# Six edits to the order of work in a transformer layer: the end of the output stage, the norm tiles, one head's queue, and the token sums

## The chip, the cores and the metric

The kernel runs on one core of a Trainium2 chip. The core has a matrix engine (PE, TensorE), three engines for element-wise work (DVE or VectorE, ACT or ScalarE, POOL or GpSimd), and SP, whose queue issues the transfers between the outer memory and the core's own. Each engine takes its instructions strictly in the order of its own queue; an instruction that waits for a result of another engine holds up everything queued behind it. The metric is the device time in microseconds (us), the median of three runs: 1238.08 for the kernel before (1235.4 to 1239.1).

## The reference

One encoder layer on a sequence of 1024 tokens of width 1024. A projection of `x` is split between four mLSTM heads (a short convolution over tokens on q and k, then a recurrent matrix memory, both directions summed) and eight windowed attention heads; the head outputs go through one output projection; a first layer norm; a gated feed-forward network (SwiGLU, inner width 2816) with a gated extra embedding; a second layer norm.

```python
mix = concat([mlstm(conv(x @ Wqk), x @ Wv), attention(x @ Waq)]) @ w_out
x   = layer_norm(ALPHA * x + mix, ln1_g, ln1_b)
ffn = (silu(x @ Wg) * (x @ Wu)) @ w_ffn_out
x   = layer_norm(ALPHA * x + ffn + sigmoid(x @ Wple_g) * (p @ Wple_p), ln2_g, ln2_b)
```

## The kernel before, in words

All products are made to fp32 accuracy from two-part operands: a high part that ACT rounds off (`split`: `act.copy`) and a low part, the rest, that POOL or DVE subtracts. `mm3` makes hi*hi, lo*hi and hi*lo into one PSUM bank, so a 128x512 product of 128x128 weights is three PE instructions. Where names below end in h and l (`mh`, `ml`, `a1h`, `a1l`, `t3h`, `t3l`) they are such parts.

The 1024 tokens are eight tiles of 128. The stages are: projections of x; attention; four mLSTM heads one after the other (each works in 128-token chunks on PE, with long chains over ACT, POOL and DVE between the products, while the PE queue is filled up with projection products of the next head); the output projection; the first norm (`ln1_*`) tile by tile, tiles 4 to 7 before 0 to 3 (`TORD`); the feed-forward network by a two-by-two block scheme with 7 products for 8, which needs sums of pairs of tiles (`t_sums`: tile t+4 += tile t; `t_sums2`: the sums of the second kind, formed from those in place, by two additions on the engine named); its output (`run_out`, `ffn_out`) and the second norm (`ln2`).

In the second norm DVE collects the statistics, POOL raises the variance to the power -1/2 (`rs`, a 128x1 instruction), DVE subtracts the mean and multiplies by the gain, and each half row is then finished either by one DVE instruction (times `rs`, plus the bias `b2b`) or by ACT (times `rs`) and POOL (plus `b2b`), and sent out by SP.

Most of the program is placed by a scheduler: it builds each engine's queue from its own estimate of when things are ready. `strict[0]` and `fixed[0]` keep a stretch in the written order, and `with tc.issue_after(ins)` puts instructions into their engine's queue behind `ins`; on the same engine that is an order and no wait. In the output stage (`ffn_out`) each block `m` is the sum of six weight pieces for four tiles; the last block (`m == 4`, tiles 0 to 3) is run tile by tile, the one before it (`m == 3`, tiles 4 to 7) piece by piece over all four.

The names that matter below: `ks` (scaled keys of a head chunk), `kp` (keys transposed by PE), `pp` (query-key product), `qk` (a convolved q or k, five DVE instructions over 1024 tokens: one TENSOR_SCALAR and four SCALAR_TENSOR_TENSOR), `hs` (a head's output chunk), `tr` (its transpose on PE), `so` (the output of a head, normed), `yo` (a PSUM bank of the output projection), `y` (a norm tile, `y_4121`, `4149`, `4169`, `4185` for tiles 0 to 3 and `3960`, `4007`, `4050`, `4085` for 4 to 7), `rg` and `ru` (raw feed-forward weights) and `x_8193` to `x_8199` (odd; output tiles 0 to 3).

Of the kernel before, what the change touches and what calls it, by code (L numbers as in the profile page):

```python
# [10 lines left out]
ALU = mybir.AluOpType  # L11
# [4 lines left out]
P = 128  # L16
D = 1024
S = 1024
# [17 lines left out]
def hybrid_layer(  # L36
# [80 lines left out]
    def pjb(name):  # L117
        return pj.tile([P, 512], F32, name=name, tag="pj")

    def flat(t):  # L120
        return t.rearrange("p a b -> p (a b)")

    def split(dst_hi, dst_lo, src, eng_lo=None):
        act.copy(dst_hi, src)
        if eng_lo == "halves":
            for c in range(2):
                cs = slice(c * 512, c * 512 + 512)
                pool.tensor_tensor(dst_lo[:, cs], src[:, cs], dst_hi[:, cs].bitcast(F32), ALU.subtract)
            return
        (eng_lo or pool).tensor_tensor(dst_lo, src, dst_hi.bitcast(F32), ALU.subtract)  # L130

    def load_w(src, shape, name, eng_lo=None, raw=None):
# [4 lines left out]
        lo = wp.tile([P] + shape, F32R, name="lo_" + name, tag="wlo", bufs=4)  # L137
        split(flat(hi), flat(lo), flat(raw), eng_lo or "halves")
        return hi, lo

    last = {}

    def mm3(o, ah, al, bh, bl, start, stop, goes_on=False):
        pe.matmul(o, ah, bh, start=start, stop=False, skip_group_check=goes_on)
# [36 lines left out]
    def drain(n=0):  # L181
        while len(fillers) + len(running) > n:
            fill(1)
# [120 lines left out]
    def qk_tile(ct):  # L304
        def evac(o, hf):
            if hf == 0:
                pre = qk["pre", ct] = prep.tile([P, S + 4], F32, name="pre", tag="pre")
                dve.memset(pre[:, 0:2], 0.0)
                dve.memset(pre[:, S + 2:S + 4], 0.0)
            pre = qk["pre", ct]  # L310
            act.copy(pre[:, 2 + hf * 512:514 + hf * 512], o)
            if hf == 1:
                y = qk[ct] = Y([P, S], F32, f"qk{ct}")
                dve.tensor_scalar(y, pre[:, 0:S], colt[:, ct, 0:1], colt[:, ct, 5:6], ALU.mult, ALU.add)
                for w in range(1, 5):
                    dve.scalar_tensor_tensor(y, pre[:, w:w + S], colt[:, ct, w:w + 1], y, ALU.mult, ALU.add)
                act.activation(y, y, AF.Silu)

        return proj_T(wqk[ct], f"qk{ct}", evac)
# [268 lines left out]
    def mlstm_head(h):  # L588
# [8 lines left out]
        for hf in range(2):  # L597
            kp_ = bank("kp", "ma")
            for cc in range(4):
                c = hf * 4 + cc  # L600
                pe.transpose(kp_[:, cc * P:(cc + 1) * P], kT[:, c * P:(c + 1) * P], ident)
            for d in range(2):
                kk = W([P, 4, P], F32, f"ks{d}{hf}", 4, "ks")
                if d == 0:
                    for cc in range(4):
                        r = col(d, hf * 4 + cc)
                        act.activation(kk[:, cc, :], kp_[:, cc * P:(cc + 1) * P], AF.Copy, scale=cWA[:, r:r + 1])
                else:
                    r = col(d, hf * 4)
                    dve.tensor_tensor(kk, kp_.rearrange("p (c k) -> p c k", k=P),  # L610
                                      cWA[:, r:r + 4].unsqueeze(2).to_broadcast([P, 4, P]), ALU.mult)
                ks[d, hf] = kk
            fillr()
        orders = (list(range(8)), list(range(7, -1, -1)))
# [137 lines left out]
    gated(MH - 1, last["mm"])  # L752
    for hf in range(2):
        finish(MH - 1, hf)
    drain()

    scope_s.close()
# [150 lines left out]
    for t in range(6):  # L908
        for nh in range(2):
            list(out_proj(t, nh, (0, 1), u, False))  # L910
            if (t, nh) in TR1:
                ln1_tr(TR1[t, nh])
            if (t, nh) == (3, 1):
                ws = [wino_w1(0, raw8), wino_w1(1, raw8f)]
                s2 = [wino_s(0, *ws[0][:2])]
                p2 = X([P, 8, P], F32R, "a20")
                split(p2[:, LO, :], p2[:, UP, :], ws[0][0][:, UP, :])
                p2 = p2[:, LO, :], p2[:, UP, :]
                s2.append(wino_s(1, *ws[1][:2]))
        if t < 5:  # L920
            ln1_norm(t)
# [218 lines left out]
    ln1_gain(7)  # L1140
    t_sums(1)
    t_sums2(0, dve)
    t_sums2(1, pool)

    def wlo(pr, sl, src, eng):
        eng.tensor_tensor(pr[1][:, sl, :], src, f32(pr[0][:, sl, :]), ALU.subtract)

    wlo(p3, UP, ru[:, LO, :], pool)
    rg1, ru1 = ws[1][:2]
    q2, q3 = w_pair(1, 2), w_pair(1, 3)  # L1150
    parts = (q2, LO, s2[1]), (q3, UP, ru1[:, LO, :]), (q2, UP, rg1[:, UP, :]), (q3, LO, ru1[:, UP, :])
# [6 lines left out]
    ob[1] = m12(1, 2, pjb("mb"))  # L1158
    t_sums(2)
    t_sums(3)  # L1160
    for t in (2, 3):
        t_sums2(t, pool)
    for part in ((p4, UP, s2[0]), (p4, LO, rg[:, LO, :]), (p3, LO, ru[:, UP, :])) + parts:
        wlo(*part, pool)
    evac([tr_pe((4, 5), 512, q) for q in range(2)], bx["t3"], 0, bdif)
# [13 lines left out]
    act.activation(hs[0][0], hs[0][0], AF.Silu)  # L1179
    oc = bank("mc", "w")  # L1180
    prod(w2[0], 5, oc, True)
    tb = tr_pe((6, 7), 512, 1)
    tr_hi(tb, 1, bx["t3"], 2, bdif)
    tr_lo(tb, 1, bx["t3"], 2, bdif)
    act.activation(hs[1][0], hs[1][0], AF.Silu)
# [164 lines left out]
        nc.sync.dma_start(xb[:, :nj, :], hb[q][HB[m]][:, :nj, :])  # L1350
        return piece(new_pair, xa, nj, f"wo{m}{q}", dve), piece(new_pair, xb, nj, f"ho{m}{q}", dve), nj

    def run_out(o, units, first, tts=range(4)):
        for ui, (a, b, nj) in enumerate(units):
            for j in range(nj):
                for tt in tts:
                    s = slice(tt * P, (tt + 1) * P)
                    mm3(o[tt], b[0][:, j, s], b[1][:, j, s], a[0][:, j, :], a[1][:, j, :],
                        first and ui == 0 and j == 0, ui == len(units) - 1 and j == nj - 1, not first)

    def ffn_out():
        for t in range(NT):
            stat[t] = W([P, 2, 6], F32, "st2", 8)
        oa = [bank(f"oa{tt}", "w") for tt in range(4)]
        ob = None
        dst = {1: (0, 0), 2: (0, 0), 6: (0, 1), 5: (1, 1), 7: (1, 1), 3: (0, 1), 4: (1, 0)}
        for m in (1, 2, 6, 5, 7, 3, 4):
            if m in (2, 5):
                ob = [pjb(f"ob{m}{tt}") if tt < 3 else bank(f"ob{m}{tt}", "w") for tt in range(4)]
            o = ob if m in (2, 5, 3) else oa  # L1370
            units = [unit(m, q) for q in range((NPR + 1) // 2)]
            first = m in (1, 2, 5)
            if m != 4:
                run_out(o, units, first)
            nh, hf = dst[m]
            for tt in range(4):
                if m == 4:
                    run_out(o, units, first, [tt])
                y, t = yv(nh, hf, tt), hf * 4 + tt
                add(y, y, o[tt])  # L1380
                if m in (2, 7, 3, 4):
                    dve.bn_stats(stat[t][:, nh, :], y)
                if m in (3, 4):
                    ln2(t)

    def ln2(t):
        y = ya[t]
        mv = W([P, 2], F32, "mv2", 4)
        rs = W([P, 1], F32, "rs2", 4)
        dve.bn_aggr(mv, stat[t])  # L1390
        dve.tensor_scalar(rs, mv[:, 1:2], LN_EPS, None, ALU.add)
        pool.tensor_tensor(rs, rs, mhalf[:, 0:1], ALU.pow)
        dve.scalar_tensor_tensor(y, y, mv[:, 0:1], g2b, ALU.subtract, ALU.mult)
        for nh in range(2):
            ns = slice(nh * 512, nh * 512 + 512)
            if t >= 4 and nh == 0 or t == 7:
                dve.scalar_tensor_tensor(y[:, ns], y[:, ns], rs, b2b[:, ns], ALU.mult, ALU.add)
            else:
                act.activation(y[:, ns], y[:, ns], AF.Copy, scale=rs)
                pool.tensor_tensor(y[:, ns], y[:, ns], b2b[:, ns], ALU.add)  # L1400
            nc.sync.dma_start(out[t * P:(t + 1) * P, ns], y[:, ns])
# [74 lines left out]
```

## Time and profile before

| quantity | us |
|---|---|
| median of three runs | 1238.08 |
| profiled execution | 1238.7 |
| span of its trace | 1236.9 |
| PE busy | 1204.0 (97%) |
| DVE busy | 843.7 (68%) |
| ACT busy | 509.9 (41%) |
| POOL busy | 405.9 (33%) |
| PE's waits for other engines, summed | 21.3 |

The span is the traced time from first to last instruction; 1.8 us of the profiled execution lie outside it. Busy shares are averages over stages; what an edit is worth has to be read at its place, from the timeline there: one line is an instruction, or several alike, with start, busy time, engine, what it writes and reads, and in brackets how long its engine stood idle before it and for whom.

### The profile page before, as it was taken

The numbers are of one execution on the slowest core, as the hardware profiler recorded it, in microseconds if no ns is written. First come the engines' busy times: TensorE is split into PE (matmuls) and PEld (weight loads), VectorE is DVE, ScalarE is ACT, GpSimd is POOL, SyncE is SP. The second block draws the span as 40 slices with busy tenths as digits, with TensorE's granted clock in tenths as the row PEclk, the third lists the DMA queues.
The fourth block names the chain that finished last, engine by engine and source line by source line (L and its number), as shares of the span: only waits on it lengthen the run. The fifth ranks groups of instructions, "written<-read, shape, count | busy, mean of one in ns | idle before, by whom it ended". The sixth has DMA issues, their size and how long they took to land.

```text
span 1236.9 us, 16505 instructions
## 1 busy us (share of the span) xinstructions
PE 1204.0 (97%) x6017; PEld 1004.4 (81%) x6017; DVE 843.7 (68%) x1543; ACT 509.9 (41%) x920; POOL 405.9 (33%) x324
## 2 busy tenths in 40 slices
PE   8999999999999999899999999999999999999996
PEld 8888888788778878788888888888887888888885
DVE  6866555867788789665857667576467696555566
ACT  5655444534662236533324334333243333333331
POOL 4542322615344034622332323323227440000017
PEclk9999999999999999999999999999999999999998
DMA  6331112313174132145545454465345556565603
GB/s 233 94 97 69 44 60 79 130 35 121 51 243 167 51 137 102 35 133 177 183 164 196 168 190 163 145 220 180 126 137 208 192 187 224 193 194 189 187 1 136
DMA packets 68785, 174.40 MB, mean 141 GB/s; under 512 B 7328, under 2 KB 12128, under 8 KB 68704
## 3 DMA queue, kind: packets, MB, share of 16 engines
q1 hardware_dynamic: 68704, 173.35, 41.1%
q8 instruction: 47, 0.77, 0.3%
q14 instruction: 34, 0.28, 0.1%
HBM read 126.86 MB, written 46.47 MB: 140 GB/s over the span
## 4 chain that ended last, share of the span: by engine, by line
PE 77%; DVE 9%; DMA 2%; issue 2%; POOL 2%; ACT 2%; POOLq 0%; SPq 0%; ACTq 0%; DVEq 0%
PE ma L73 19%; PE mc L73 9%; PE oa L73 7%; PE ob L73 7%; PE pj_qk L73 6%; PE mb L73 4%; PE pg L73 4%; PE yo L73 3%; PE pn_v L73 3%; PE pj_o L73 2%; PE pj_aq L73 2%; PE op L73 2%; PE nd L73 2%; PE et L77 1%; PE sp L73 1%
## 5 line engine op out<-in xcount | busy, mean ns | idle before, releaser
L57 POOL TENSOR_TENSOR rs<-rs,mhalf 128x1 f32<-128x1 f32 (+1 forms) x24 | 22.0, 917 | 250.2 <-DVE rs L57 242.0
L57 POOL TENSOR_TENSOR s<-ru,rg 128x512 f32<-128x512 f32 x20 | 26.8, 1342 | 188.3 <-DMA ru<-in_wffi_dram 188.3
L57 POOL TENSOR_SCALAR e<-e,st 128x384 f32<-128x384 f32 (+1 forms) x64 | 35.0, 560 | 93.8 <-DVE st L57 54.8
L57 DVE TENSOR_TENSOR us<-us,ma 128x512 f32<-128x512 f32 x22 | 15.0, 683 | 68.3 <-PE ma L73 68.3
L73 PE MATMUL yo<-hi_wo,mh 128*128 128x512 f32 x128 | 51.5, 402 | 2.7 <-DVE y L57 2.7
L57 DVE SCALAR_TENSOR_TENSOR qk<-pre,colt,qk 128x1024 f32<-128x1024 f32 x32 | 52.4, 1636 | 0.6
L73 PE MATMUL pj_qk<-xh,hi_qk 128*128 128x512 f32 x128 | 51.5, 402 | 0.0
L73 PE MATMUL pj_qk<-xl,hi_qk 128*128 128x512 f32 x128 | 50.7, 396 | 0.0
L73 PE MATMUL pj_qk<-xh,lo_qk 128*128 128x512 f32 x128 | 50.6, 396 | 0.0
L73 PE MATMUL yo<-lo_wo,mh 128*128 128x512 f32 x128 | 50.2, 392 | 0.0
L73 PE MATMUL yo<-hi_wo,ml 128*128 128x512 f32 x128 | 49.7, 392 | 0.0
L57 ACT CAST a4h<-s 128x512 fp32r<-128x512 f32 x21 | 13.1, 622 | 84.5 <-POOL s L57 42.9
L57 POOL TENSOR_TENSOR s<-rg,s 128x512 f32<-128x512 f32 x20 | 26.4, 1320 | 56.1 <-DVE a4l L57 56.1
L57 ACT CAST a2h<-s 128x512 fp32r<-128x512 f32 x41 | 24.4, 619 | 49.2 <-PE mc L73 31.3
L57 DVE CUSTOM_DVE_ANT_0 e<-sp,bias 128x384 f32<-128x384 f32 (+1 forms) x64 | 31.2, 521 | 19.7 <-PE sp L73 17.8
L57 POOL TENSOR_TENSOR s<-ru 128x512 f32<-128x512 f32 x20 | 34.2, 1709 | 23.4 <-DVE a2l L57 23.4
L57 ACT ACTIVATE e<-e,st 128x384 f32<-128x384 f32 (+1 forms) x64 | 37.2, 583 | 8.3 <-DVE st L57 8.3
L57 ACT COPY eT<-et 128x384 f32<-128x384 f32 (+1 forms) x32 | 14.4, 450 | 54.5 <-PE et L77 54.4
L57 DVE TENSOR_TENSOR yb<-yb,us 128x512 f32<-128x512 f32 x22 | 36.3, 1651 | 0.0
L57 ACT ACT_TABLE_LOAD x25 | 32.1, 1283 | 9.1 <-DMA mw<-mwd 7.1
L73 PE MATMUL mc<-t1h,a3h 128*128 128x512 f32 x88 | 34.4, 391 | 0.8 <-DVE t1l L57 0.8
L73 PE MATMUL mb<-b21h,a1h 128*128 128x512 f32 x88 | 34.3, 390 | 0.0
(890 smaller groups left out, 4161.1 us busy)
## 6 DMA issues: line engine op xcount, KB each, us to landing
fb<-hb SPq DMA_DIRECT2D x35, 512.0 KB, 4.5
rg<-in_wffi_dram SPq DMA_DIRECT2D x22, 512.0 KB, 3.6
ru<-in_wffi_dram SPq DMA_DIRECT2D x22, 512.0 KB, 5.2
fa<-sb SPq DMA_DIRECT2D x20, 512.0 KB, 3.4
mw<-mwd SPq DMA_DIRECT2D x16, 512.0 KB, 5.3
fa<-in_wffo_dram SPq DMA_DIRECT2D x15, 512.0 KB, 3.8
hb<-yc SPq DMA_DIRECT2D x11, 512.0 KB, 2.9
hb<-ya SPq DMA_DIRECT2D x11, 512.0 KB, 3.7
```

Source lines behind the costliest of these rows:

```text
L57: self.ins = op(*args, **kw)
L73: return pe.put(nc.tensor.matmul(*args, **kw))
L77: return pe.put(nc.tensor.transpose(*args, **kw))
```

## The change: six edits

1. The cast of the first feed-forward weights (`a1h`, in `wino_w1`) is put into ACT's queue behind the last head's last cast (`mh`).
2. The five convolution instructions of the third `qk` tile are put into DVE's queue behind the last scale of keys (`ks`) of the first head that DVE makes.
3. The second kind of token sums of tile 1 goes from POOL to DVE; on POOL those of tile 3 come first, then one low part of weights (`p3`), then those of tile 2.
4. One group of transposes (`tr_pe((6,7),512,1)`) gets its PSUM bank from another pool.
5. In the last but one output block (`m == 3`) the last two of its six weight pieces are run tile by tile, so that the four tiles end one after the other.
6. In the second norm tile 3 is finished wholly on DVE and tiles 0 to 2 in their first half; tiles 4 to 7 wholly on ACT and POOL.

```diff
     def split(dst_hi, dst_lo, src, eng_lo=None):
-        act.copy(dst_hi, src)
+        last["hi"] = act.copy(dst_hi, src)
...
                 y = qk[ct] = Y([P, S], F32, f"qk{ct}")
-                dve.tensor_scalar(y, pre[:, 0:S], colt[:, ct, 0:1], ...)
-                for w in range(1, 5):
-                    dve.scalar_tensor_tensor(y, pre[:, w:w + S], ...)
+                with tc.issue_after(last["ks"].ins) if ct == 2 else ExitStack():
+                    (the same five instructions)
...
-                    dve.tensor_tensor(kk, kp_...)
+                    last["ks"] = dve.tensor_tensor(kk, kp_...)
...
     for hf in range(2):
         finish(MH - 1, hf)
+    last["mh"] = last["hi"]
...
-                ws = [wino_w1(0, raw8), wino_w1(1, raw8f)]
+                with tc.issue_after(last["mh"].ins):
+                    ws = [wino_w1(0, raw8), wino_w1(1, raw8f)]
...
-    t_sums2(1, pool)
+    t_sums2(1, dve)
...
-    wlo(p3, UP, ru[:, LO, :], pool)
...
-    for t in (2, 3):
-        t_sums2(t, pool)
+    t_sums2(3, pool)
+    wlo(p3, UP, ru[:, LO, :], pool)
+    t_sums2(2, pool)
...
-    tb = tr_pe((6, 7), 512, 1)
+    tb = tr_pe((6, 7), 512, 1, "x1s")
...
-            if m != 4:
+            if m == 3:
+                run_out(o, units[:-2], first, ends=False)
+            elif m != 4:
                 run_out(o, units, first)
...
-                if m == 4:
-                    run_out(o, units, first, [tt])
+                if m in (3, 4):
+                    run_out(o, units[-2:] if m == 3 else units, first, [tt])
...
-            if t >= 4 and nh == 0 or t == 7:
+            if t == 3 or t < 3 and nh == 0:
                 dve.scalar_tensor_tensor(y[:, ns], y[:, ns], rs, b2b[:, ns], ALU.mult, ALU.add)
```

The instruction order shows three places. First DVE's queue in the first mLSTM head, before and after; `ks_2384` and `ks_2402` are the head's two scales of keys on DVE, `qk_2483` is the tile that is moved, `C_2372` the head's memory, `mw` a masked query-key product:

```order
397 L57 TENSOR_SCALAR qk_2483<-pre,colt 128x1024
398 L57 SCALAR_TENSOR_TENSOR qk_2483<-pre,colt,qk_2483 128x1024 x2
399 L57 TENSOR_TENSOR ks_2384<-kp,gcol 128x512
400 L57 SCALAR_TENSOR_TENSOR qk_2483<-pre,colt,qk_2483 128x1024
401 L57 TENSOR_TENSOR ks_2402<-kp,gcol 128x512
402 L57 SCALAR_TENSOR_TENSOR qk_2483<-pre,colt,qk_2483 128x1024
403 L57 COPY C_2372<-up 128x129
```

```order
397 L57 TENSOR_TENSOR ks_2384<-kp,gcol 128x512
398 L57 TENSOR_TENSOR ks_2402<-kp,gcol 128x512
399 L57 TENSOR_SCALAR qk_2483<-pre,colt 128x1024
400 L57 SCALAR_TENSOR_TENSOR qk_2483<-pre,colt,qk_2483 128x1024
401 L57 COPY C_2372<-up 128x129
402 L57 SCALAR_TENSOR_TENSOR qk_2483<-pre,colt,qk_2483 128x1024
403 L57 SCALAR_TENSOR_TENSOR mw_2506<-pp,mw_2506 128x4x128
```

Both scales now stand ahead of the convolution, and two of its five instructions move behind the rows of the head's own chain. The scheduler also places much of the three following heads anew on all engines.

Second, ACT's queue at the start of the output projection (`hi_wo` are its weights, `y_4121` and `y_4149` norm tiles):

```order
289 L57 CAST hi_wo_4343<-raw_wo_4341 128x1024
290 L57 CAST hi_wo_4349<-raw_wo_4347 128x1024
291 L57 CAST a1h_4558<-rg_4554 128x1024
292 L57 CAST mh_4107<-so_3844 128x512
293 L57 ACTIVATE y_4121<-y_4121,rs_4385 128x512 x2
```

```order
288 L57 CAST hi_wo_4343<-raw_wo_4341 128x1024
289 L57 CAST hi_wo_4349<-raw_wo_4347 128x1024
290 L57 CAST mh_4107<-so_3844 128x512
291 L57 CAST a1h_4558<-rg_4554 128x1024
292 L57 ACTIVATE y_4121<-y_4121,rs_4385 128x512 x2
```

The two casts have changed places. Third, the end of POOL's queue, where `rs` is the power for one tile and `x` the additions of the bias for tiles 0 to 3 in turn:

```order
241 L57 TENSOR_TENSOR rs_10253<-rs_10253,mhalf 128x1
242 L57 TENSOR_TENSOR rs_10300<-rs_10300,mhalf 128x1
243 L57 TENSOR_TENSOR x_8193<-x_8193,b2b 128x512 x2
244 L57 TENSOR_TENSOR x_8195<-x_8195,b2b 128x512 x2
245 L57 TENSOR_TENSOR rs_10347<-rs_10347,mhalf 128x1
246 L57 TENSOR_TENSOR x_8197<-x_8197,b2b 128x512 x2
247 L57 TENSOR_TENSOR rs_10394<-rs_10394,mhalf 128x1
248 L57 TENSOR_TENSOR x_8199<-x_8199,b2b 128x512 x2
```

```order
240 L57 TENSOR_TENSOR rs_10258<-rs_10258,mhalf 128x1
241 L57 TENSOR_TENSOR x_8193<-x_8193,b2b 128x512
242 L57 TENSOR_TENSOR rs_10304<-rs_10304,mhalf 128x1
243 L57 TENSOR_TENSOR x_8195<-x_8195,b2b 128x512
244 L57 TENSOR_TENSOR rs_10350<-rs_10350,mhalf 128x1
245 L57 TENSOR_TENSOR x_8197<-x_8197,b2b 128x512
246 L57 TENSOR_TENSOR rs_10396<-rs_10396,mhalf 128x1
```

Eight additions have become three, and none stands behind the last power. On DVE two half-row instructions for `x_8199` are added behind its gain instruction, at the queue's end.

## Rows read from the trace of the kernel before

**Rows 1.** The page's first line.
```profile
span 1236.9 us, 16505 instructions
```

**Rows 2.** PE's waits: total us, times, longest us.
```profile
PE tr L77 <- DVE hs L57: 4.5, 3, 1.9
...
PE yo L73 <- DVE y L57: 2.7, 3, 1.7
PE x1t L77 <- DVE t3l L57: 2.3, 3, 1.1
PE pp L73 <- DVE ks L57: 2.2, 2, 1.1
```

**Rows 3.** Timeline of the end: start us, busy us, engine, operation, [idle before <-releaser].
```profile
1204.66 0.74 DVE L57 SCALAR_TENSOR_TENSOR x<-x,rs,b2b 128x512 f32<-128x512 f32 x1
...
1208.82 1.77 DVE L57 SCALAR_TENSOR_TENSOR x<-x,rs,b2b 128x512 f32<-128x512 f32 x1
...
1226.60 3.47 POOL L57 TENSOR_TENSOR x<-x,b2b 128x512 f32<-128x512 f32 x2 [0.83 <-ACT x L57]
...
1227.33 1.62 DVE L57 SCALAR_TENSOR_TENSOR x<-x,mv,g2b 128x1024 f32<-128x1024 f32 x1
1230.03 0.54 POOL L57 TENSOR_TENSOR rs<-rs,mhalf 128x1 f32<-128x1 f32 x1
1230.61 1.33 ACT L57 ACTIVATE x<-x,rs 128x512 f32<-128x512 f32 x2 [3.47 <-POOL rs L57]
1231.41 2.48 POOL L57 TENSOR_TENSOR x<-x,b2b 128x512 f32<-128x512 f32 x2 [0.83 <-ACT x L57]
```

**Rows 4.** Timeline in the first head, around the moved convolution.
```profile
229.99 4.42 DVE L57 SCALAR_TENSOR_TENSOR qk<-pre,colt,qk 128x1024 f32<-128x1024 f32 x2
...
232.04 1.13 ACT L57 ACTIVATE ks<-kp,gcol 128x128 f32<-128x128 f32 x4
...
234.33 0.68 DVE L57 TENSOR_TENSOR ks<-kp,gcol 128x512 f32<-128x512 f32 x1
...
235.07 1.16 PE L73 MATMUL pp<-qk,qk 128*128 128x128 f32 x8 [1.12 <-DVE ks L57]
```

**Rows 5.** Timeline in the second head.
```profile
314.35 3.16 DVE L57 TENSOR_SCALAR hs<-hs,mv,rs 128x128 f32<-128x128 f32 x4 [1.14 <-POOL rs L57]
...
317.05 0.73 PE L77 MATMUL tr<-ident,hs 128*128 128x128 f32 x2 [1.91 <-DVE hs L57]
```

**Rows 6.** Stretches: length us; busy us (count) of PE, PEld, DVE, ACT, POOL; granted clock; DMA share, GB/s.
```profile
300.00:312.00 12.00, 12.00 (x57) 9.80 (x55) 12.00 (x22) 4.38 (x12) 8.20 (x6) 1.00 0.59 176
...
318.00:320.00 2.00, 2.00 (x8) 1.71 (x8) 2.00 (x6) 1.11 (x4) 0.00 (x0) 0.50 0.64 246
```

**Rows 7.** Timeline at the output projection.
```profile
437.75 1.05 ACT L57 CAST a1h<-rg 128x1024 fp32r<-128x1024 f32 x1 [3.50 <-DMA rg<-in_wffi_dram]
...
438.70 0.61 ACT L57 CAST mh<-so 128x512 fp32r<-128x512 f32 x1
...
439.35 1.36 DVE L57 TENSOR_TENSOR ml<-so,mh 128x512 fp32r<-128x512 f32 x1 [1.52 <-ACT mh L57]
...
441.36 0.50 PE L73 MATMUL yo<-hi_wo,mh 128*128 128x512 f32 x1 [1.65 <-DVE y L57]
...
444.29 1.28 DVE L57 SCALAR_TENSOR_TENSOR y<-y,yo 128x512 f32<-128x512 f32 x2 [1.82 <-DMA y<-in_xn_dram]
```

**Rows 8.** Timeline of the token sums, DVE, POOL and PE.
```profile
493.09 1.61 POOL L57 TENSOR_TENSOR y<-y,y 128x512 f32<-128x512 f32 x1 [4.18 <-DVE y L57]
493.59 1.66 DVE L57 TENSOR_TENSOR y<-y 128x512 f32<-128x512 f32 x1
...
498.84 0.68 DVE L57 TENSOR_TENSOR y<-y 128x512 f32<-128x512 f32 x1
...
499.55 1.67 DVE L57 TENSOR_TENSOR y<-y,y 128x512 f32<-128x512 f32 x1
...
502.15 0.63 PE L77 MATMUL x1t<-ident,y 128*128 128x128 f32 x4 [1.09 <-DVE t3l L57]
```

More of the change, by code (lines that the diff above doesn't have):

```diff
@@ L118, in pjb @@
         return pj.tile([P, 512], F32, name=name, tag="pj")
+    last = {}
     def flat(t):
@@ L139, in load_w @@
         return hi, lo
-    last = {}
     def mm3(o, ah, al, bh, bl, start, stop, goes_on=False):
@@ L313, in evac @@
                 y = qk[ct] = Y([P, S], F32, f"qk{ct}")
-                dve.tensor_scalar(y, pre[:, 0:S], colt[:, ct, 0:1], colt[:, ct, 5:6], ALU.mult, ALU.add)
-                for w in range(1, 5):
-                    dve.scalar_tensor_tensor(y, pre[:, w:w + S], colt[:, ct, w:w + 1], y, ALU.mult, ALU.add)
+                with tc.issue_after(last["ks"].ins) if ct == 2 else ExitStack():
+                    dve.tensor_scalar(y, pre[:, 0:S], colt[:, ct, 0:1], colt[:, ct, 5:6], ALU.mult, ALU.add)
+                    for w in range(1, 5):
+                        dve.scalar_tensor_tensor(y, pre[:, w:w + S], colt[:, ct, w:w + 1], y, ALU.mult, ALU.add)
                 act.activation(y, y, AF.Silu)
@@ L609, in mlstm_head @@
                     r = col(d, hf * 4)
-                    dve.tensor_tensor(kk, kp_.rearrange("p (c k) -> p c k", k=P),
-                                      cWA[:, r:r + 4].unsqueeze(2).to_broadcast([P, 4, P]), ALU.mult)
+                    last["ks"] = dve.tensor_tensor(kk, kp_.rearrange("p (c k) -> p c k", k=P),
+                                                   cWA[:, r:r + 4].unsqueeze(2).to_broadcast([P, 4, P]), ALU.mult)
                 ks[d, hf] = kk
@@ L1351, in unit, with run_out @@
         return piece(new_pair, xa, nj, f"wo{m}{q}", dve), piece(new_pair, xb, nj, f"ho{m}{q}", dve), nj
-    def run_out(o, units, first, tts=range(4)):
+    def run_out(o, units, first, tts=range(4), ends=True):
         for ui, (a, b, nj) in enumerate(units):
@@ L1358, in run_out @@
                     mm3(o[tt], b[0][:, j, s], b[1][:, j, s], a[0][:, j, :], a[1][:, j, :],
-                        first and ui == 0 and j == 0, ui == len(units) - 1 and j == nj - 1, not first)
+                        first and ui == 0 and j == 0, ends and ui == len(units) - 1 and j == nj - 1, not first)
     def ffn_out():
```

## The prediction, made before the changed kernel was run

> **What bounds the kernel now.** I read the span first: 1236.9 us [rows 1], in a profiled execution of 1238.7, so 1.8 lie outside it and the execution stands 0.6 above the median of 1238.08. All sums below go against 1238.7. 0.3% of the time, 3.7 us, is about what a measurement of this kernel can tell from no change.
>
> PE is busy nearly throughout, so a change can win only where PE stands still or after its last product. The view of PE's waits says where it stands [rows 2]: the reader is to see that four of its lines, `tr` for `hs`, `yo` for `y`, `x1t` for `t3l` and `pp` for `ks`, are waits for DVE, 11.7 us together, and that each falls into a stage that an edit touches. The stretch after the last product is not in that view; it is read in the timeline of the end [rows 3].
>
> **The end (edits 5 and 6).** POOL runs the two bias additions of tile 2 from 1226.60 for 3.47, to 1230.07. Only then comes the last power at 1230.03, although DVE had started the gain instruction of tile 3 at 1227.33 and so had the variance by then [rows 3]. ACT scales both halves from 1230.61, and POOL's last two additions end at 1231.41 + 2.48 = 1233.89. That is the last piece of work, 3.0 before the span's end; these 3.0 are the transfer out and stay.
>
> After the change no addition stands between the powers of tiles 2 and 3 but one, that of tile 2, and none after the last. Tile 3's power can run beside the gain instruction. I expect that instruction at 1.3 instead of 1.62, ending by 1228.6, and two half-row instructions behind it at 0.66 to 0.74 each, as the one at 1204.66 did [rows 3], ending at 1229.9 instead of 1233.89: -4.0. Bounds: if POOL's one addition for tile 2 still runs beside them, they take 1.62 and twice up to 1.77, as the row at 1208.82 did, and end at 1232.5: -1.4. If all is quick, -4.6. I take -4.0 since tile 2's single addition should start with ACT's half at once, before tile 3's statistics are there.
>
> The price is that tiles 4 to 7 put eight additions and four powers on POOL. From the last row but one of the end an addition is 1.24 to 1.74, so about 16 us with the powers. Edit 5 pays for that: the four tiles end 9 products apart instead of together, so the first of them comes to POOL well before the last. With some 16 us of products still ahead for tiles 0 to 3 a backlog of a few us at tile 0 is worked off beside them, since each of tiles 0 to 2 now brings POOL one addition and not two. The pieces of `m == 3` also free their buffers later, by the time of those products, for the casts of the last block; ACT is idle there for much of the time, so I cost it at nothing. If that cover is gone, PE waits once, for no longer than 9 products take.
>
> **The convolution behind the scales (edit 2), where it is made.** DVE runs two convolution instructions of 2.21 each from 229.99, and one scale `ks` only at 234.33 [rows 4]. PE stands 1.12 at `pp` for it, and again about as long before the next group: 2.2 in two waits [rows 2]. ACT's scales, the other half, end at 233.17 [rows 4]. With DVE's scales first, the later of the two is ACT's, and PE, which reaches the group at 233.95, finds all there: -2.2. Bounds: 0, if another chain is late at the same place, to -2.2. The convolution itself ends about as before, since it is the same five instructions less the two scales in between.
>
> **What the edit does to the rest of the heads.** The scheduler places three heads anew. In PE's new order the transposes `tr` and products that depend on `hs` stand some 13 to 32 products further back than before, while in DVE's order the work that feeds them hardly moves. So PE comes later to the same waits, and the 4.5 us of `tr` [rows 2] should shrink. Against that stands that DVE is full just there: 12.00 of 12.00 us in 300 to 312 [rows 6]. Where DVE is the limit, PE being ahead only lengthens the wait. I take -1.5 for this (one in three of the 4.5), with -4 (nearly all of it) and +3 (a new wait as long as the one at 313 to 317, [rows 5]) as bounds.
>
> The clock comes into this. PE stood 1.1 and then 1.91 before 317.05 [rows 5], and in 318 to 320 the granted clock was 0.50 [rows 6], the level of 1.2 GHz, which costs 1.0 us in these 2 us and some 1.6 with the flanks. The Trainium skill, "TensorE: Matmul & The Clock Gate", section "Why this matters for your kernels", says that idle gaps between bursts throw the engine back to half its clock, and the trace agrees here (0.50 after 3.0 us of idle). By that rule the shortening of these gaps returns a further 1.6 us, and a new gap of that length in a later head would cost as much again.
>
> **The output projection (edit 1).** ACT's cast `a1h` waits 3.50 for its transfer and holds the queue until 438.80; `mh` goes behind it at 438.70, and DVE's `ml`, idle 1.52 for it, takes 1.36 from 439.35 because POOL subtracts `a1l` at the same time [rows 7]. The sum of `y` behind it keeps PE idle 1.65 before 441.36, and the transfer of the next `y` also starts behind `ml`, so that DVE waits 1.82 for it before 444.29 [rows 7]. All three `yo` waits make 2.7 [rows 2]. With `mh` first it runs 0.95 to 1.5 earlier, and `ml` takes 0.68 as a plain subtraction of that size does (498.84, [rows 8]): the chain is 1.6 to 2.2 earlier. PE's 1.65 shrinks to the round trip of the sum, about 0.7, and the last wait closes: -1.5, bounds -0.6 and -2.2. `a1h` and what follows on ACT move 0.6 later; nothing there is needed within a few us.
>
> **The token sums (edits 3 and 4).** Between 493 and 501 POOL adds `y` while DVE does the same sort of sums, and three of DVE's take 1.45 to 1.67 (the first at 493.59, the last at 499.55) instead of 0.68 [rows 8]: 2.7 us lost. The Trainium skill, "GPSIMD Engine Reference", section "Key points", says that POOL shares its memory interfaces with DVE and collides with DVE instructions that have two such inputs; the trace agrees (1.66 against 0.68). By the same rule the half rows that edit 6 moves to DVE are exposed too, but only while POOL adds; that is the bound of -1.4 above.
>
> Two sums move to DVE, 2 x 0.68 = 1.36, and POOL's come only after DVE's: DVE's list ends 2.7 - 1.36 = 1.3 earlier. PE's wait for `t3l` there is 1.09 [rows 8], followed by one set by ACT's `t1h`, so I count -1.0. Edit 4 frees a bank and removes one of three `x1t` waits of 2.3 together [rows 2], but ACT's casts that follow are late by as much: 0. POOL's chain behind it (`p3`, then the sums of tile 2, then the low parts) runs about 1.3 later, and the first low part has about 1 us of room. Bounds: +1.5 (that part is late) to -2.3.
>
> **Sum.** -4.0 (end) - 2.2 (`pp`) - 1.5 (other heads) - 1.5 (output projection) - 1.0 (token sums) = -10.2, so 1238.7 - 10.2 = 1228.5; I say 1228.5. All the low bounds together would give 1238.7 - 4.6 - 2.2 - 4 - 2.2 - 2.3 = 1223.4, all the high ones 1238.7 - 1.4 + 0 + 3 - 0.6 + 1.5 = 1241.2.
>
> **Rivals.**
> A. The gain in the heads is given back. DVE, not PE, sets the time from 300 on (12.00 of 12.00 [rows 6]), so that PE, 2.2 earlier, only waits longer at `hs`. For it speaks that row, against it that PE reaches the `tr` groups later in the new order. Time: 1238.7 - 4.0 - 1.5 - 1.0 = 1232.2.
> B. The heads give back, and the end wins only half, because POOL is still busy with the eight additions of tiles 4 to 7 when tile 0 comes and DVE's half rows wait for powers. For it: POOL's backlog in the last 20 us before. Against: it has only three additions of tiles 0 to 2 left. Time: 1238.7 - 1.4 - 1.5 - 0.6 = 1235.2, no change that can be told.
> C. Slower: the new order of the heads makes DVE's chain for `hs` late at PE in each of the three later heads, with a gap as in rows 5 and the clock at half speed behind it [rows 6], 3.0 + 1.6 = 4.6 each time. The known gap stays, and three new ones cost 13.8: 1238.7 - 6.5 (end, output projection, sums) + 13.8 - 2.2 = 1243.8. It decides from two and a half new gaps on; two give 1239. What speaks for it is that the scheduler, and no trace, made that order; against it, that products for PE have moved in front of the waits.
> D. Edit 4 or 3 does what it says, but POOL's first low part is late and PE waits for it: 1238.7 - 10.2 + 2.5 = 1231.0.
>
> **How the numbers follow.** My forecast has 0.42, A 0.24, D 0.08, B 0.15, C 0.11. The forecast (1224 to 1231.5 by itself), A and D are faster by over 3.7, less a small part of A that ends near the bound: 0.73. B and the mild form of C are no change: 0.18. C in full is slower: 0.09. The range is 1223.4, all low bounds, to 1239, where two of C's gaps would put it; all the high bounds at once are left out with C in full.
>
> **What would show it.** Right: the last power starts within 1 us of the gain instruction of tile 3, DVE and not POOL does the last piece, and it ends about 4 us nearer to the last product. The line `pp` for `ks` is gone from PE's waits. At the output projection `mh` stands before `a1h`, and the `yo` line falls from 2.7 to near 1. DVE's sums between 493 and 501 take 0.68 each. Wrong: the `tr` or `nd` lines of PE's waits grow beyond 7 us, or a new stretch with a granted clock of 0.5 stands in the heads; POOL still adds when tile 3's variance is there; or the start of the feed-forward products stands less than 4 us earlier than before.

## The result, and the profile after

The changed kernel takes 1225.49 us (median of four runs, 1225.12 to 1227.77), the kernel before 1238.19 on the same chip: a ratio of 0.9902, 95% interval 0.9882 to 0.9921. The forecast was 1228.5 in a range of 1223.4 to 1239. The span of the profiled execution fell by 12.9, from 1236.9 to:

```profile
span 1224.0 us, 16509 instructions
```

Because PE runs the same long groups of products in both, the start times of such groups, as the view of the critical chain lists them, cut the span into stages. `yo x24` is a group in the middle of the output projection (420.57 before, 413.18 after), `yo x48` its last stretch (445.03, 436.64), `ma x26` the start of the regular feed-forward products (527.51, 518.19), `pg` the gate (949.38, 939.75), and the last product starts at 1225.14 and 1215.52.

| stage | before | after | change | forecast |
|---|---|---|---|---|
| start, attention, heads, to yo x24 | 420.57 | 413.18 | -7.39 | -3.7 (edit 2) |
| to yo x48 | 24.46 | 23.46 | -1.00 | -1.5 (edit 1) |
| to ma x26 | 82.48 | 81.55 | -0.93 | -1.0 (edits 3, 4) |
| to pg | 421.87 | 421.56 | -0.31 | 0 |
| to the last product | 275.76 | 275.77 | 0.01 | 0 |
| to the end | 11.76 | 8.48 | -3.28 | -4.0 (edits 5, 6) |

PE's waits after the change (total us, times, longest), beside [rows 2]:

```profile
PE yo L73 <- DVE y L57: 4.2, 5, 1.9
PE tr L77 <- DVE hs L57: 1.9, 2, 1.6
...
PE x1t L77 <- DVE yb L57: 0.9, 1, 0.9
...
PE x1t L77 <- DVE t3l L57: 0.2, 1, 0.2
```

The line `pp` for `ks` is gone and `tr` has lost 2.6 of its 4.5. But `yo` has grown from 2.7 to 4.2, where I had it near 1: two of its five waits are new, and the other three make 1.8.

In the first head the timeline reads as forecast, against [rows 4]:

```profile
230.78 0.69 DVE L57 TENSOR_TENSOR ks<-kp,gcol 128x512 f32<-128x512 f32 x1 [7.67 <-ACT ks L57]
...
232.61 1.05 PE L73 MATMUL pp<-qk,qk 128*128 128x128 f32 x8
232.96 0.69 DVE L57 TENSOR_TENSOR ks<-kp,gcol 128x512 f32<-128x512 f32 x1 [1.49 <-ACT ks L57]
```

Both scales stand ahead of the convolution, DVE now waits for ACT's scales instead, and PE starts `pp` without a wait. In the second head PE still waits for `hs`, but once, and the clock stays up, against [rows 5, 6]; below are two rows of the timeline and three stretches (columns as in [rows 6]):

```profile
313.27 3.15 DVE L57 TENSOR_SCALAR hs<-hs,mv,rs 128x128 f32<-128x128 f32 x4
...
315.96 0.59 PE L77 MATMUL tr<-ident,hs 128*128 128x128 f32 x2 [1.61 <-DVE hs L57]
```

```profile
300.00:312.00 12.00, 12.00 (x70) 10.46 (x69) 10.24 (x26) 5.70 (x13) 5.52 (x6) 1.00 0.54 176
...
316.00:318.00 2.00, 2.00 (x11) 1.63 (x12) 1.96 (x4) 0.94 (x4) 0.00 (x0) 1.00 0.49 96
318.00:320.00 2.00, 2.00 (x10) 1.66 (x9) 1.96 (x4) 1.97 (x3) 0.00 (x0) 1.00 0.41 166
```

`hs` came 1.1 earlier than before (313.27 against 314.35), and PE, which had stood 3.0 in two waits there, stood 1.61. The granted clock is 1.00 where it was 0.50. DVE, full in 300 to 312 before, is busy for 10.24 of the 12.00 there. For the next output PE waited 1.52 at 360.80 before and does not wait now (357.95); DVE's row for it, before and after:

```profile
355.87 5.13 DVE L57 TENSOR_SCALAR hs<-hs,mv,rs 128x128 f32<-128x128 f32 x4 [0.15 <-POOL rs L57]
```

```profile
354.30 1.12 DVE L57 TENSOR_SCALAR hs<-hs,mv,rs 128x128 f32<-128x128 f32 x4 [0.17 <-POOL rs L57]
```

Where the new `yo` waits come from is read at the end of the heads:

```profile
387.45 1.29 POOL L57 TENSOR_TENSOR mw<-mw,maskb 128x512 f32<-128x512 f32 x1 [9.35 <-DMA mw<-mwd]
...
391.17 1.31 POOL L57 TENSOR_TENSOR mw<-qk,mw 128x512 f32<-128x512 f32 x1
...
392.51 0.33 SPq L740 DMA_DIRECT2D y<-in_xn_dram  x1
...
396.11 0.69 DVE L57 SCALAR_TENSOR_TENSOR y<-y,yo 128x512 f32<-128x512 f32 x1 [0.37 <-DMA y<-in_xn_dram]
...
396.85 0.50 PE L73 MATMUL yo<-hi_wo,mh 128*128 128x512 f32 x1 [1.86 <-DVE y L57]
```

POOL stood 9.35 for the transfer of a masked product; the transfer of a `y` tile is issued 0.03 after POOL's last use of `qk` ends, and 3.6 later DVE can add and PE gets its bank back. PE reached this point earlier and gave some of the lead back.

At the output projection, against [rows 7], the two casts have changed places and the subtraction takes 0.69 instead of 1.36:

```profile
429.87 0.62 ACT L57 CAST mh<-so 128x512 fp32r<-128x512 f32 x1 [3.01 <-DVE so L57]
430.45 1.06 ACT L57 CAST a1h<-rg 128x1024 fp32r<-128x1024 f32 x1
430.53 0.69 DVE L57 TENSOR_TENSOR ml<-so,mh 128x512 fp32r<-128x512 f32 x1
...
433.07 0.50 PE L73 MATMUL yo<-hi_wo,mh 128*128 128x512 f32 x1 [0.78 <-DVE y L57]
```

PE's 1.65 became 0.78. At the token sums, against [rows 8], DVE's sums take 0.68 to 0.69 each, and POOL starts only behind them:

```profile
489.18 0.68 DVE L57 TENSOR_TENSOR y<-y 128x512 f32<-128x512 f32 x1
...
491.23 0.69 DVE L57 TENSOR_TENSOR y<-y,y 128x512 f32<-128x512 f32 x1
491.84 1.66 DVE L57 SCALAR_TENSOR_TENSOR t3l<-x1t,bdif,t3h 128x256 fp32r<-128x256 f32 x4
492.06 1.28 POOL L57 TENSOR_TENSOR y<-y,y 128x512 f32<-128x512 f32 x1 [11.07 <-DVE y L57]
```

The end, against [rows 3]:

```profile
1215.52 0.39 PE L73 MATMUL oa<-wo45hi,ho45lo 128*128 128x512 f32 x1
...
1217.78 1.28 DVE L57 SCALAR_TENSOR_TENSOR x<-x,mv,g2b 128x1024 f32<-128x1024 f32 x1
1218.01 1.46 POOL L57 TENSOR_TENSOR rs<-rs,mhalf 128x1 f32<-128x1 f32 x1 [2.58 <-DVE rs L57]
1219.50 1.41 DVE L57 SCALAR_TENSOR_TENSOR x<-x,rs,b2b 128x512 f32<-128x512 f32 x2 [0.44 <-POOL rs L57]
```

The power starts 0.23 behind the gain instruction and not 2.7 behind it, and DVE does the last work. But the power takes 1.46 here, against 0.54 before, when DVE was idle beside it; the half rows wait 0.44 for it.

### The profile page after: what moved, and what is told of

Its sections match the earlier page's. It is cut to its first block, busy times and chain, and to the rows that moved or that the text cites. A ratio compares the mean times of both kernels' runs of the same rounds, so it can differ in the third digit from the quotient of the medians.

```text
span 1224.0 us, 16509 instructions
## 1 busy us (share of the span) xinstructions
PE 1201.1 (98%) x6017; PEld 1003.4 (82%) x6017; DVE 833.0 (68%) x1545; ACT 508.1 (42%) x919; POOL 399.6 (33%) x322
## 4 chain that ended last, share of the span: by engine, by line
PE 87%; DVE 5%; DMA 3%; ACT 2%; issue 2%; POOL 1%; POOLq 0%; SPq 0%; DVEq 0%; ACTq 0%
PE ma L73 19%; PE oa L73 10%; PE mc L73 10%; PE ob L73 7%; PE mb L73 5%; PE pj_qk L73 5%; PE yo L73 4%; PE pg L73 4%; PE pj_aq L73 3%; PE pn_v L73 3%; PE pj_o L73 3%; PE nd L73 2%; PE op L73 2%; PE sp L73 2%; PE et L77 1%
## 5 line engine op out<-in xcount | busy, mean ns | idle before, releaser
L57 DVE SCALAR_TENSOR_TENSOR qk<-pre,colt,qk 128x1024 f32<-128x1024 f32 x32 | 48.0, 1501 | 0.6
```

Source lines behind the costliest of these rows:

```text
L57: self.ins = op(*args, **kw)
```

## The experiments

Times are ratios to the kernel before on the same chip, with 95% intervals, where the run was timed; the waits and stages are from the trace of one execution each. First the edits one by one (edits 1, 2 and 6 each alone, 3 and 4 together, 5 only together with 6). The diffs are shortened; `...` marks what is left out.

**Edit 2 alone.** The kernel before with

```diff
+                with tc.issue_after(last["ks"].ins) if ct == 2 else ExitStack():
                     (the five convolution instructions)
...
-                    dve.tensor_tensor(kk, ...)
+                    last["ks"] = dve.tensor_tensor(kk, ...)
```

> The kernel before with the second edit alone (convolution of the third qk tile behind the head's two scales of keys). Theory: this edit, with the new placing of the heads that it causes, brings most of the 12.9 us of span between the two traces: by the landmark yo at 420.9 before, 413.5 after, 7.4 us. It should then be 6 to 9 us faster than before, with the line pp for ks gone and the idle at tr near 316 at about 1.6 with no stretch at half clock. Rival: the gain in the heads hangs on the other edits too (casts after the last head, which change what ACT and the transfers do); then it is under 4 us faster.

Measured: 0.9959 (0.9945 to 0.9973), 5.1 us (3.3 to 6.8), which decides neither for the 6 to 9 of the theory nor for the rival's under 4; the span is 5.7 shorter. `yo` x24 starts at 415.16. Its early waits, up to 73, were 1.9 longer than those of before (7.07 against 5.17; these differ from one execution to the next), so by these two traces the heads themselves gained about 7.3. The one wait at `tr` is 1.59, there is no half clock in the heads, and the waits at `yo` of 1.82 and 0.56 are there too. So the waits of the changed kernel in the heads come with this edit alone, new ones included.

**Edits 5 and 6 alone.**

```diff
-            if m != 4:
+            if m == 3:
+                run_out(o, units[:-2], first, ends=False)
+            elif m != 4:
...
-                if m == 4:
-                    run_out(o, units, first, [tt])
+                if m in (3, 4):
+                    run_out(o, units[-2:] if m == 3 else units, first, [tt])
...
-            if t >= 4 and nh == 0 or t == 7:
+            if t == 3 or t < 3 and nh == 0:
```

> The kernel before with the fifth and sixth edits alone (last but one output block ended tile by tile, norm shares moved). Theory: the stretch from the last product to the end falls by 3.3 us as between the two traces (11.8 to 8.5), nothing else moves: 3 to 4 us faster. Rival: part of the 3.3 hangs on the earlier start of the output stage; then under 2 us.

Measured: 0.9983 (0.9968 to 0.9999), 2.1 us (0.1 to 4.0), too wide to tell 3.3 from the rival's under 2. In the trace it takes 8.52 from the last product (1226.08) to the end of the span, as after, 3.24 less than before. The stage gives its 3.3 whatever stands ahead of it.

**Edit 1 alone.**

```diff
-        act.copy(dst_hi, src)
+        last["hi"] = act.copy(dst_hi, src)
...
+    last["mh"] = last["hi"]
...
-                ws = [wino_w1(0, raw8), wino_w1(1, raw8f)]
+                with tc.issue_after(last["mh"].ins):
+                    ws = [wino_w1(0, raw8), wino_w1(1, raw8f)]
```

> The kernel before with the first edit alone (cast of feed-forward weights behind the last head's cast on ACT). Theory: PE's waits at yo between 436 and 446 fall from 2.7 to 1.8 (as after), so 1.0 us faster, at the edge of what can be told from no change. Rival: by the prediction's sum 1.5 us. Second rival: the casts that follow are late and it is no faster.

Measured: 0.9999 (0.9987 to 1.0011), no change that can be told. In the trace the `yo` waits are 1.8 instead of 2.7, and `yo` x24 to x48 took 23.51 instead of 24.46. The stage shrank as after; whether the whole time did, this run can't tell.

**Edits 3 and 4 alone.**

```diff
-    t_sums2(1, pool)
+    t_sums2(1, dve)
...
-    wlo(p3, UP, ru[:, LO, :], pool)
...
-    for t in (2, 3):
-        t_sums2(t, pool)
+    t_sums2(3, pool)
+    wlo(p3, UP, ru[:, LO, :], pool)
+    t_sums2(2, pool)
...
-    tb = tr_pe((6, 7), 512, 1)
+    tb = tr_pe((6, 7), 512, 1, "x1s")
```

> The kernel before with the third and fourth edits alone (token sums, bank of one transposition). Theory: PE's waits between 498 and 512 fall from 3.1 to about 1.8 and DVE's sums take 0.68 each: 0.9 to 1.3 us faster. Rival: only the wait moves (the bank's to yb), 0.

Measured: 0.9994 (0.9981 to 1.0008), inconclusive as a time. In the trace the stage from `yo` x48 to `ma` took 81.95 instead of 82.48, with a wait of 0.5 at 480.9 that the traces of before and after don't have (the second one of the changed kernel, below, has it with 0.6); without it the stage is 1.05 shorter, within the 0.9 to 1.3 expected.

**Edit 6 without edit 5.**

```diff
-            if t >= 4 and nh == 0 or t == 7:
+            if t == 3 or t < 3 and nh == 0:
```

> The kernel before with the sixth edit alone (norm shares moved, blocks still ended together). Theory: POOL now has eight additions of tiles 4 to 7 from 1203 on, as they come late and together, and is still at them when tiles 0 and 1 come; each of tiles 0 to 2 brings one addition, so the backlog is gone by tile 3 and the stretch from last product to end is 8.5 as in the changed kernel. Rival: without the fifth edit the backlog reaches tile 3 and the stretch stays above 10.

Measured, in one execution: from the last product to the end of the span 10.2 (1224.21 to 1234.4). My theory was wrong and the rival right. The timeline of that kernel's end:

```profile
1219.87 0.55 POOL L57 TENSOR_TENSOR rs<-rs,mhalf 128x1 f32<-128x1 f32 x1
1220.39 2.99 POOL L57 TENSOR_TENSOR x<-x,b2b 128x512 f32<-128x512 f32 x2
1220.45 0.72 ACT L57 ACTIVATE x<-x,rs 128x512 f32<-128x512 f32 x1 [2.73 <-POOL rs L57]
1220.46 1.78 DVE L57 SCALAR_TENSOR_TENSOR x<-x,rs,b2b 128x512 f32<-128x512 f32 x1 [1.69 <-POOL rs L57]
...
1226.37 0.68 DVE L57 TENSOR_TENSOR x<-x,oa 128x512 f32<-128x512 f32 x1
...
1229.91 1.42 DVE L57 SCALAR_TENSOR_TENSOR x<-x,rs,b2b 128x512 f32<-128x512 f32 x2 [0.44 <-POOL rs L57]
```

POOL is behind by its additions for tiles 4 to 7, DVE's half row of each tile waits for its power, and behind that half row stands the next tile's addition from PSUM. So the backlog goes from POOL into DVE's queue, and tile 3's addition, which could start at about 1224.6, starts at 1226.37. Edit 6 alone gives half of the 3.3, and edit 5 on top of it the other half, as the prediction had it (edit 5 pays for edit 6); edit 5 without edit 6 was not run.

**All but edit 2.** The changed kernel without `issue_after(last["ks"].ins)`.

```diff
-                with tc.issue_after(last["ks"].ins) if ct == 2 else ExitStack():
                     (the five convolution instructions stay)
```

> The changed kernel without the second edit. Theory: its heads are those of before, with the stretch at half clock near 320 (1.7 us) and the waits at pp, tr, nd and up; the sum of the other edits' stages is 0.8 + 0.9 + 3.3 = 5.0, so 5 us faster than before, 1233.3. Rival: edits 1, 3 and 4 bring nothing without the lead from the heads, and only the end's 3.3 remain: 1235.

Measured: 0.9949 (0.9931 to 0.9967), 1233.25, where the theory had 1233.3. By the ratio that is 6.3 us (4.1 to 8.5), so the theory's 5.0 holds and the rival's 3.3 does not; in the trace the stages gave 0.9, 1.3 and 3.3. The other five edits' stages add up without the heads.

Two traces alone overstate the heads. In the six traces with the heads of before `yo` x24 starts at 419.3 to 421.5, in the three with edit 2 as in the changed kernel at 413.2 to 415.2: 6.3 by the means, where the first pair gave 7.4. As a time edit 2 is worth 5.1 alone and 4.7 to 5.8 with the others (0.9949 against 0.9911 and 0.9902).

So the question is why the heads gave 5 to 6 and not 3.7, and whether that hangs on this one list. In the next kernels only edit 2's rule is varied, or one thing that makes the scheduler place the heads anew; all have the other five edits.

**Behind the first scale only.**

```diff
-                    last["ks"] = dve.tensor_tensor(kk, ...)
+                    ins = dve.tensor_tensor(kk, ...)
+                    last.setdefault("ks", ins)
```

> The changed kernel, but the convolution of the third qk tile stands behind the first of the head's two scales of keys only, not behind both. The scheduler places the later heads again in another way. Theory (the gain in the heads is mostly the later heads' new places, and these are a matter of how the scheduler's list happens to fall): pp for ks shows one wait of about 1 us, and the waits in the later heads (300 to 400) differ from the changed kernel's by several us either way. Rival (the gain comes from DVE being free of the convolution early, and PE's lead is simply kept): one wait of 1 us more, and the rest as in the changed kernel, 1 to 1.3 us slower than it.

Measured: 0.9975 (0.9962 to 0.9987), 1236.15, 8 to 9 us more than the changed kernel by the ratios (0.9911 and 0.9902). PE's wait at `pp` is 0.64 instead of 2.2, but others have come:

```profile
PE up L73 <- DVE C L57: 3.8, 4, 1.6
PE yo L73 <- DVE y L57: 3.3, 3, 1.6
PE nd L73 <- DVE C L57: 1.7, 1, 1.7
```

and behind four waits close together at 400 to 406 the clock is down (PE's columns only: length, busy, granted clock, transfers):

```profile
400.00:410.00 10.00, 6.11 (x18) 0.67 0.71 242
```

The rival, that PE's lead is simply kept, is refuted: the first head was as good but for 0.6, and most was lost at the end of the last head.

**A second tile, in the second head, and in the third.**

```diff
-                with tc.issue_after(last["ks"].ins) if ct == 2 else ExitStack():
+                with tc.issue_after(last["ks"].ins) if ct in (2, 4) else ExitStack():
```

> The changed kernel with the same rule for a second tile: the convolution of the fifth qk tile too is queued behind the second head's scales of keys. Theory (a matter of how the list falls): heads between 3 us faster and 4 us slower than the changed kernel. Rival (freeing DVE for the scales is good in each head): 1 to 2 us faster, as the wait for hs at 314 to 316 (1.6) goes.

Measured: 0.9971 (0.9957 to 0.9984), 1235.57, by the ratios 7 to 9 us slower than the changed kernel, so beyond the theory's 4, and the rival is refuted. And with `ct in (2, 6)`, whose second convolution stands behind the scales of the third head:

```diff
-                with tc.issue_after(last["ks"].ins) if ct == 2 else ExitStack():
+                with tc.issue_after(last["ks"].ins) if ct in (2, 6) else ExitStack():
```

> The changed kernel with the rule for the third and the seventh qk tile. The list is the same up to the third head. Theory (a matter of how the list falls): the first two heads as in the changed kernel, the third and fourth between 2 us faster and 6 us slower. Rival (freeing DVE for the scales is good in each head): 0.5 to 1.5 us faster.

Measured: 1.0015 (1.0001 to 1.0029), 1240.15, the changed kernel's whole gain gone, beyond the 6 us that I had as the worst. Its waits, two stretches (PE's columns), and DVE and PE in the third head:

```profile
PE pj_o L73 <- ACT pre L57: 4.9, 1, 4.9
...
PE up L73 <- DVE C L57: 2.9, 1, 2.9
PE tr L77 <- DVE mw L57: 2.2, 1, 2.2
```

```profile
320.00:330.00 10.00, 4.00 (x28) 0.76 0.28 105
330.00:340.00 10.00, 8.14 (x38) 0.72 0.01 2
```

```profile
323.29 0.32 DVE L57 SCALAR_TENSOR_TENSOR C<-C,gcol,up 128x129 f32<-128x129 f32 x1
...
323.67 1.27 DVE L57 SCALAR_TENSOR_TENSOR qk<-pre,colt,qk 128x1024 f32<-128x1024 f32 x1
324.86 0.34 DVE L57 SCALAR_TENSOR_TENSOR C<-C,gcol,up 128x129 f32<-128x129 f32 x1
...
325.25 1.66 PE L73 MATMUL up<-va,ks 128*128 128x129 f32 x6 [2.91 <-DVE C L57]
```

The `up` line shows what a late convolution does to the head: its instructions of 1.27 each stand in DVE's queue between the updates of the head's memory `C`, and PE waits 2.9 for one of these. In the kernel with tiles 3 and 5 the same wait is 2.7, at 276.97.

A line stands first that the changed kernel has only with 0.3: a projection waits for ACT's copy into `pre`, the input of the convolution, so that PE doesn't get its PSUM bank back. In the kernel with tiles 3 and 5 this wait is 1.8, and the late convolution is the cause: in ACT's queue the copy stands behind the SiLU of that convolution.

```profile
278.14 1.06 ACT L57 ACTIVATE qk<-qk 128x1024 f32<-128x1024 f32 x1 [10.54 <-DVE qk L57]
279.11 0.57 ACT L57 COPY pre<-pj_qk 128x512 f32<-128x512 f32 x1
...
279.73 0.79 PE L73 MATMUL pj_o<-xh,hi_o 128*128 128x512 f32 x1 [1.82 <-ACT pre L57]
```

The 4.9 with tiles 3 and 7 is only in part of that kind. There the convolution ends at 326.54, before PE begins to wait. ACT first stands 9.22 for a masked product `mw` from POOL, which had stood 11.87 for its transfer; from 327.69 on it scales that product, loads a table and runs the SiLU, and the copy ends at 331.81. So freeing DVE for the scales is not good in each head: in the first it costs 0.3 at this line, later it holds up the head's own chain.

**The fifth tile instead of the third.**

```diff
-                with tc.issue_after(last["ks"].ins) if ct == 2 else ExitStack():
+                with tc.issue_after(last["ks"].ins) if ct == 4 else ExitStack():
```

> The changed kernel with the rule for the fifth qk tile instead of the third. The first head is then as before: pp waits 2.2 for ks. Theory: these 2.2 us are back, and the later heads fall in some other way, so 2 to 9 us slower than the changed kernel. Rival (freeing DVE for the scales is good in each head, and 2.2 is all that is lost): 0 to 2 us slower.

Measured: 0.9939 (0.9916 to 0.9962), 1232.87, 4.2 slower than the changed kernel beside it (1228.72, below), as the theory had it. `pp` waits 2.5 (2.2 before); it is no better than without the rule (0.9949).

**Five buffers for `mw`.**

```diff
-                mw = W([P, 4, 2, P], F32, f"mw{h}{hf}{d}", 4, "mw")
+                mw = W([P, 4, 2, P], F32, f"mw{h}{hf}{d}", 5, "mw")
```

> The changed kernel with five buffers instead of four for the masked products mw, whose transfers make POOL wait 9.35 at 387 and so hold up the y tile for yo at 397. Theory (a matter of how the list falls): the heads, placed anew once more, lose several us against the changed kernel, 3 to 10 us slower than it. Rival (buffers set the late waits): the yo waits of 1.9 and 0.6 go and it is 1 to 2.5 us faster than the changed kernel.

Measured: 0.9908 (0.9887 to 0.9929), as fast as the changed kernel, so neither expectation holds. The first `yo` wait fell from 1.86 to 0.25, as the rival said, but `tr` waits rose from 1.9 to 2.5 and an `up` wait of 0.7 came, and the sum stayed.

**The changed kernel again.** No edit.

> The changed kernel once more, beside the other kernels of this call. Theory: its list is the same, so the heads again show only the waits at tr near 316 (1.6) and yo near 397 (1.9 and 0.6) and no stretch at half clock, and it is again 1.0% faster than before (12 us). Rival: the missing half-clock stretch was a chance of one execution; then it shows one as before does (1.7 us) and is near 1227.

Measured: 0.9911 (0.9890 to 0.9931), 1228.72 on another chip than the first. The waits in the heads are nearly the same, but this execution had a stretch at half clock, 1.7 us, behind a `yo` wait of 1.80; the first trace has the same wait with 1.86 and no such stretch. A row of the timeline and two stretches (PE's columns):

```profile
396.12 0.50 PE L73 MATMUL yo<-hi_wo,mh 128*128 128x512 f32 x1 [1.80 <-DVE y L57]
```

```profile
396.00:398.00 2.00, 1.88 (x6) 0.67 0.85 225
398.00:400.00 2.00, 2.00 (x6) 0.50 0.35 102
```

So the missing stretch of the first trace is partly chance, as the rival said.

Put together, by the waits of PE for other engines between 230 and 412 and what the granted clock cost there (length of a stretch times what its clock lacks of 1), each from one trace; the times are medians, and the kernel before had 1238.2 beside the changed kernel, 1239.1 beside "all but edit 2", "first scale only" and "tiles 3 and 5", and 1238.1 beside the others:

| kernel | waits | clock | time |
|---|---|---|---|
| before | 9.1 | 1.7 | 1238.2 |
| all but edit 2 | 8.7 | 3.4 | 1233.3 |
| changed | 4.7 | 0 | 1225.5 |
| changed, again | 4.5 | 1.7 | 1228.7 |
| five `mw` buffers | 4.5 | 1.7 | 1228.5 |
| tile 5 instead | 7.3 | 3.4 | 1232.9 |
| first scale only | 8.3 | 3.4 | 1236.2 |
| tiles 3 and 5 | 8.9 | 3.4 | 1235.6 |
| tiles 3 and 7 | 11.9 | 6.8 | 1240.2 |

Below its first row the times differ by 14.7; less the two sums they are 1220.8 to 1224.5. So these lists differ in time mainly by PE's waits in the heads and the clock behind them.

## Why the prediction was right, step by step

- *The `pp` wait, -2.2.* Right, in place, size and cause.
- *The rest of the heads, -1.5, bounds -4 and +3.* Right way, but the mechanism held only in part and the size did not. I had PE coming later to the waits for `hs` while DVE's work hardly moves. The waits shrank, but near 315 PE came only 0.3 later (at 314.35, against 315.14 less the 1.11 that it had just waited) and `hs` 1.1 earlier; at the next output PE came 1.3 earlier and found `hs` ready, which took DVE 1.12 with POOL idle and had taken 5.13 beside POOL, at work without a pause from 355.81 to 360.67. So it was mostly DVE that came earlier; how much of that POOL's new place gave was not tested. To the `yo` group the stage gave 7.39, so the rest gave 5.2, beyond my bound; by the means of nine traces it gave 6.3, the rest 4.1, at the bound. Waits explain 4.4 in all with `pp` in it (9.1 to 4.7, new `yo` waits of 2.4 counted) and the clock 1.7; about 1.3 of the 7.39 lie in no listed wait and stay open. That is within what executions differ by: the start of the last product, less PE's waits and what the clock cost, is 1198.4 to 1202.5 in the fourteen traces, 1202.1 before and 1200.9 after. I had named the clock's 1.6 in sentences beside the sum and left it out of the sum: by the first trace it belonged in. By the second trace of the same kernel, which has a stretch of its own, it did not.
- *Rival A, the heads give it back.* Wrong for this list, since PE waited only 1.6 at the place I had named; right for two others that free the first scales as well (first scale only; tiles 3 and 5), where the gain was given back elsewhere. My reason, DVE full in 300 to 312, did not last: in the new order DVE is busy for 10.24 of the 12.00. Where PE waits depended on how the later rows fell.
- *Rival B, half of the end lost to POOL's backlog.* Not here, but it is what edit 6 does without edit 5: DVE's half rows wait 1.69 for powers, and the end gains 1.6 instead of 3.3.
- *Rival C, slower.* Not here. But the kernel with tiles 3 and 7 has C's form: three long waits and the clock behind them, 1240.2, though PE waits there for `C`, a copy and `mw` and not for `hs`. What I priced at 0.09 was one list away.
- *Rival D, POOL's first low part late.* Wrong: no wait of PE for POOL stands in the view of waits.
- *The output projection, -1.5.* Right way, -1.0: the casts and `ml` came as much earlier as worked out, and PE's 1.65 became 0.78, but the last `yo` wait stayed at 0.55 since the transfer still lands late (DVE waits 1.71 for it).
- *The token sums, -1.0.* Right, -0.93, with the sums at 0.69 each. The bank's wait (1.06) turned into one for `yb` (0.90), so edit 4 gave next to nothing, as forecast; edits 3 and 4 were not run apart.
- *The end, -4.0.* Right way, -3.28. Of the 0.7 missing, 0.44 is the half rows' wait for the power: I let it run beside the gain instruction at its 0.54 and it took 1.46. I had applied the collision of POOL and DVE to POOL's additions only. The Trainium skill, "GPSIMD Engine Reference", section "Key points", says what collides with POOL are DVE instructions with two inputs in the core's own memory (SBUF); the gain instruction is one, and the trace agrees (1.46 against 0.54).

The total was right partly by luck, by sizes that were off in both directions: the small edits gave 1.3 less than forecast, the heads 3.7 more by the first pair of traces and 2.6 more by the means. Of the signs that I had named, one of being right failed, since the `yo` line grew, and one of being wrong appeared in the second trace, a new stretch at 0.50 in the heads.

## What to carry to other kernels

When an edit makes a scheduler place a long stretch anew, the wait it was made for can be forecast and the rest can't: five lists that differ in one rule gave 1225 to 1240. Price such an edit with its own wait, keep the spread wide, and measure each neighbouring list, since the same rule for one more tile can take back everything. Small edits in stretches of fixed order add up nearly as worked out (5.2 of 6.5 here), and the stage times of one trace show them where a time with a 0.15% interval can't. A stage that the scheduler placed, and that holds waits and clock stretches, needs several traces: one pair gave 7.4 here, the means 6.3.

## What the runs showed of the hardware

POOL's power on a 128x1 tile takes 0.54 with DVE idle and 1.46 while DVE runs a 128x1024 SCALAR_TENSOR_TENSOR, although it is on another engine and tiny. In the output stages of the fourteen traces every power that stood beside a SCALAR_TENSOR_TENSOR of DVE, with its two inputs in SBUF, ended 0.40 to 0.42 behind the end of that instruction, whenever it had begun (for tiles 2 and 3 of the changed kernel 1213.33 behind 1212.92 and 1219.47 behind 1219.06); all others took 0.54 to 0.56, the one beside a DVE instruction with a single input too, in the trace of edit 6 alone:

```profile
1207.93 0.69 DVE L57 BATCH_NORM_STATS2 st<-x 128x6 f32<-128x512 f32 x1
...
1208.41 0.55 POOL L57 TENSOR_TENSOR rs<-rs,mhalf 128x1 f32<-128x1 f32 x1
```

The reverse shows in the heads: DVE's four `hs` instructions (128x128 TENSOR_SCALAR) took 1.11 to 1.12 with POOL idle (at 397.63 and 416.72 before, at 354.30 and 393.49 after) and 2.07 to 5.13 where POOL worked beside them (at 377.02 and 355.87 before).

And the granted clock fell to 0.50, the level of 1.2 GHz, behind short waits: behind 1.1 and 1.9 with one product between them [rows 5], and in the repeated run behind a single one of 1.80. It did not fall behind the 1.61 at 315.96, nor behind the 1.86 at 396.85, the same wait of the same kernel in its first trace. So the length of a wait alone did not decide it. The loss in the heads was 0 or 1.7 for the changed kernel, 1.7 or 3.4 with the heads of before, and 6.8 at most. The Trainium skill, "TensorE: Matmul & The Clock Gate", section "Why this matters for your kernels", warns of idle gaps between bursts of products; the traces agree, with gaps as short as these.
